# Reciprocal square roots by a power on GpSimd in a two-block transformer kernel

## The chip, the core and the metric

The kernel runs on one core of a Trainium2 chip, as one launch. The core has five engines, each with an instruction queue of its own that is worked off in order: TensorE (PE: matmuls and transposes into PSUM), VectorE (DVE), ScalarE (ACT), GpSimd (POOL) and SyncE (SP, which issues the DMAs). An instruction that needs another engine's result waits for it on a semaphore, and everything behind it in the same queue waits too. The metric is the device time in microseconds, the median of several runs.

## What is computed

One sequence of 256 tokens with 1024 features passes two blocks in float32. The first block puts 16 learned tokens ahead and mixes by a gated convolution branch and a sparse attention branch, followed by an FFN with a short convolution:

```python
h = rms_norm(stream, mix_norm_g[l])
...
y_a = conformer_conv_branch(u_conv, conv_ln_g[l], conv_ln_b[l], conv_dw_w[l], ...)   # has a layer norm
y_b = dsa_sparse_attention(q, k, v, q_idx, k_idx, w_idx, attn_w_o[l])
stream = stream + (g_a * y_a + g_b * y_b) @ w_merge_out[l]
h = rms_norm(stream, ffn_norm_g[l])
...
out = rms_norm(stream, final_norm_g)
```

The second block has two layers. The first mixes by gated linear attention (GLA: four heads, each with a norm of its own over 256 features), the second by block attention (MoBA). Each mixer and each FFN is added to a scaled stream and followed by a layer norm, so there are four of those:

```python
def layer_norm_2(x, g, b, eps=1e-5):
    xf = x.astype(jnp.float32)
    mu = jnp.mean(xf, -1, keepdims=True)
    var = jnp.mean(jnp.square(xf - mu), -1, keepdims=True)
    return ((xf - mu) * lax.rsqrt(var + eps) * g + b).astype(x.dtype)
```

Every norm thus needs 1/sqrt(v + eps) for one number per token (or per token and head).

## The kernel before

**Matmuls.** Each float32 matmul is split into a high and a low part of both factors, and three products are summed (high-high, high-low, low-high). The weights stream in chunks of 1 MB: SP issues their DMAs into three raw buffers (L111), ScalarE rounds each half chunk to its high part (`whi`, L134), DVE subtracts to get the low part (`wlo`, L136, 306 times). Activations stand transposed (features on partitions) in `hT_h` and `hT_l`; a norm's result is transposed on PE by `to_T` (L256, its PE line is L260), four 128x128 pieces at a time, copied out by ScalarE as the high part (L263) and subtracted by DVE for the low part (L266). `xs_late` (L836) is a projection that takes the high part's products first (L840, L841) and those with the low part last (L843), so that it can start before the low part is there.

**Order.** A scheduler sets the order of each engine's instructions by priorities and an estimate of when their inputs are there. Inside `tc.manual_schedule` the order on DVE and ScalarE is that of the code instead; the order on PE is the scheduler's everywhere. For the four layer norms of the second block the order is written out in the table `ORDER` (L65 to L70), one string each. An upper-case letter is a step on token tile 0, a lower-case one on tile 1: A adds stream and mixer (L742), S takes statistics of a half (L745), G joins them to mean and variance, adds epsilon and starts the root (L754, L755 and the first three rows of the iteration), C centres a half and multiplies by the gain (L749: y, the mean and the row `lg`), N is one Newton step, F finishes a half (times the root, plus the row `lb`, L761) and issues its transposes, L takes a low part (L266), x starts the next projection, t loads a ScalarE table, k lets weight splits go on. Digits are halves of 512 features.

**The root.** `rsqrt_steps` (L232) works on DVE: a shift and a subtraction of the integer bits give a first guess (L235, L236), L237 halves the negative argument, and three Newton steps refine it, each of two instructions for one column (L241, L245) or three for more columns (L243 to L245): 9 or 12 instructions of at most 128x3 numbers. It is used 17 times:
- at the start for the input norm, three columns (L307, L308); its readers scale the two token tiles on DVE (L311, L312) and ScalarE (L313), and PE transposes them;
- in `rstd_row` (L567), for the norm behind the convolution and for the FFN norm: PE sums over features (L572), DVE adds epsilon (L574), the root is taken (L575) and PE transposes it to a row (L578);
- in the final norm of the first block, once for each token tile (L714, L715); its reader L720 scales a half straight out of PSUM, and `to_T` follows;
- four times in the GLA mixer, two heads each (L1017, L1018), read by L1021;
- in the four layer norms, twice each.

## Time and profile before

| | |
|---|---|
| time, median of 3 runs | 1108.08 us (1105.93, 1108.08, 1108.15) |
| span of the profiled execution | 1106.3 us |
| PE busy | 1086.0 us (98%) |
| DVE busy | 767.1 us (69%) |
| ScalarE busy | 595.8 us (54%) |
| GpSimd busy | 0.2 us, four instructions |
| HBM read | 182.91 MB, 166 GB/s over the span |

The profile shows one execution. The page gives no time of its own for it besides the span; the median of the runs is 1.8 us above the span. Busy time counts an engine's instructions; PE's are pipelined, so that a start is more exact than an end. In a timeline the bracket behind a row is the time in which its engine had nothing to do before it, with the instruction that ended that wait.

### The profile page before, as it was taken

What the parts mean: (1) busy time and instruction counts of PE and PEld (TensorE: products, weight loads), DVE (VectorE), ACT (ScalarE), POOL (GpSimd) and SP (SyncE); (2) the same over time, 40 slices, a digit from 0 to 9 for tenths busy, and PEclk for the clock granted to TensorE, in tenths of its full rate; (3) what the DMA queues carried; (4) which work ended last, traced back from release to release, by engine and by line L of the source; (5) the groups of instructions that cost most, each with busy time, mean ns of one, the idle gap of its engine ahead of it and who ended that gap; (6) DMA issues with size and microseconds to landing.
All of it is one profiled execution on the core that took longest, in us unless ns stands there. A gap on an engine that the chain in (4) does not pass through costs nothing.

```text
span 1106.3 us, 17667 instructions
## 1 busy us (share of the span) xinstructions
PE 1086.0 (98%) x7022; PEld 972.8 (88%) x7022; DVE 767.1 (69%) x1494; ACT 595.8 (54%) x1049; POOL 0.2 (0%) x4
## 2 busy tenths in 40 slices
PE   8999999999999999999999999999999999999996
PEld 7999888999999999977877899999878878999995
DVE  6899999885677676865677745557675677555556
ACT  7785577664455555656452544446166925444440
POOL 0000000000000000000000000000000000000000
PEclk8999999999999999999999999999999999999999
DMA  7643136264265455545424555557264336555531
GB/s 279 242 145 124 45 111 212 93 211 154 94 210 190 161 199 178 187 162 177 162 94 173 195 188 188 190 191 265 78 228 153 142 125 228 191 182 183 180 141 39
DMA packets 27797, 185.10 MB, mean 167 GB/s; under 512 B 3473, under 2 KB 3857, under 8 KB 6466
## 3 DMA queue, kind: packets, MB, share of 16 engines
q1 hardware_dynamic: 27714, 183.97, 47.7%
q8 instruction: 55, 0.90, 0.3%
q14 instruction: 28, 0.23, 0.1%
HBM read 182.91 MB, written 1.05 MB: 166 GB/s over the span
## 4 chain that ended last, share of the span: by engine, by line
PE 88%; DVE 8%; ACT 2%; issue 1%; DMA 0%; SPq 0%; DVEq 0%; ACTq 0%
PE ps_wk L178 11%; PE ps_wk L179 11%; PE ps_wk L177 11%; PE ps_acc L183 10%; PE ps_acc L185 10%; PE ps_acc L184 10%; PE ps_acc L199 4%; PE ps_acc L177 3%; PE ps_acc L179 3%; PE ps_acc L178 3%; DVE wlo L136 1%; PE ps_wk L260 1%; PE ps_wk L511 1%; DVE yc L370 1%; PE ps_acc L840 1%
## 5 line engine op out<-in xcount | busy, mean ns | idle before, releaser
L136 DVE TENSOR_TENSOR wlo<-wraw,whi 128x1024 fp32r<-128x1024 f32 x306 | 371.5, 1223 | 209.6 <-ACT whi L134 208.9
L134 ACT ACTIVATE whi<-wraw 128x1024 fp32r<-128x1024 f32 x308 | 322.5, 1060 | 306.6 <-PE ps_wk L178 120.3
L178 PE MATMUL ps_wk<-hT_l,whi 128*128 128x256 f32 (+1 forms) x976 | 275.3, 282 | 0.0
L179 PE MATMUL ps_wk<-hT_h,wlo 128*128 128x256 f32 (+1 forms) x976 | 275.0, 282 | 0.0
L177 PE MATMUL ps_wk<-hT_h,whi 128*128 128x256 f32 (+1 forms) x976 | 274.3, 281 | 0.0
L177 PEld LDWEIGHTS ps_wk<-hT_h,whi 128*128 128x128 f32 x976 | 184.7, 189 | 1.0
L179 PEld LDWEIGHTS ps_wk<-hT_h,wlo 128*128 128x128 f32 x976 | 185.0, 190 | 0.4
L178 PEld LDWEIGHTS ps_wk<-hT_l,whi 128*128 128x128 f32 x976 | 184.1, 189 | 1.4
L183 PE MATMUL ps_acc<-whi,rg_h 128*128 128x512 f32 x328 | 131.5, 401 | 0.0
L184 PE MATMUL ps_acc<-wlo,rg_h 128*128 128x512 f32 x328 | 129.4, 394 | 0.0
L185 PE MATMUL ps_acc<-whi,rg_l 128*128 128x512 f32 x328 | 126.7, 394 | 0.0
L185 PEld LDWEIGHTS ps_acc<-whi,rg_l 128*128 128x128 f32 x328 | 61.6, 188 | 15.5 <-DVE rg_l L208 0.2
L183 PEld LDWEIGHTS ps_acc<-whi,rg_h 128*128 128x128 f32 x328 | 61.7, 188 | 13.7 <-ACT rg_h L206 0.2
L184 PEld LDWEIGHTS ps_acc<-wlo,rg_h 128*128 128x128 f32 x328 | 61.6, 188 | 12.7
L183 PE MATMUL ps_acc<-whi,hT_h 128*128 128x512 f32 (+1 forms) x184 | 71.5, 389 | 0.0
L185 PE MATMUL ps_acc<-whi,hT_l 128*128 128x512 f32 (+1 forms) x184 | 70.9, 385 | 0.0
L184 PE MATMUL ps_acc<-wlo,hT_h 128*128 128x512 f32 (+1 forms) x184 | 70.7, 384 | 0.0
L177 PE MATMUL ps_acc<-hT_h,whi 128*128 128x272 f32 (+2 forms) x240 | 69.3, 289 | 0.0
L178 PE MATMUL ps_acc<-hT_l,whi 128*128 128x272 f32 (+2 forms) x240 | 68.5, 286 | 0.0
L179 PE MATMUL ps_acc<-hT_h,wlo 128*128 128x272 f32 (+2 forms) x240 | 68.4, 285 | 0.0
L370 DVE SCALAR_TENSOR_TENSOR yc<-hp,dwh,yc 128x258 f32<-128x258 f32 (+14 forms) x140 | 60.8, 474 | 0.1
L368 ACT ACTIVATE z<-hp,dwh 128x258 f32<-128x258 f32 (+16 forms) x100 | 45.4, 498 | 14.5 <-DVE yc L372 10.9
(941 smaller groups left out, 1663.1 us busy)
## 6 DMA issues: line engine op xcount, KB each, us to landing
wraw<-in_wts_dram SPq DMA_DIRECT2D x166, 1024.0 KB, 4.9
lg<-in_rows_dram SPq DMA_DIRECT2D x4, 512.0 KB, 3.9
lb<-in_rows_dram SPq DMA_DIRECT2D x4, 512.0 KB, 3.9
x<-in_x_dram SPq DMA_DIRECT2D x2, 512.0 KB, 4.2
wraw<-in_wts_dram SPq DMA_DIRECT2D x2, 512.0 KB, 7.0
out_dram<-x SPq DMA_DIRECT2D x4, 256.0 KB, 2.0
mraw<-in_misc_dram SPq DMA_DIRECT2D x1, 576.0 KB, 12.7
tabs<-in_cst_dram SPq DMA_DIRECT2D x1, 544.0 KB, 12.0
```

Of the source, the lines that this page charges most:

```text
L134: A.activation(hi, r, AF.Copy)
L136: V.tensor_sub(lo, r, hi.bitcast(F32))
L177: PE.matmul(ps, wh, xh, start=first, stop=False)
L178: PE.matmul(ps, wh, xl, start=False, stop=False)
L179: PE.matmul(ps, wl, xh, start=False, stop=last)
L183: PE.matmul(ps, xh, wh, start=first, stop=False)
L184: PE.matmul(ps, xh, wl, start=False, stop=False)
L185: PE.matmul(ps, xl, wh, start=False, stop=last)
L199: PE.matmul(ps, w[:, k * P:(k + 1) * P], xT[2][:, k, a:b], start=k == 0, stop=k == KT - 1)
L260: PE.transpose(pt[:, a, :], src[:, k * P:(k + 1) * P], ident)
L368: A.activation(z[:, b, :], src[:, b, :], AF.Copy, scale=wc)
L370: V.scalar_tensor_tensor(dst[:, b, :], src[:, b, :], wc, dst[:, b, :], op0=OP.mult, op1=OP.add)
```

## The change

One function `rsqrt` takes the place of the iteration. DVE adds epsilon (with the factor 1/n where the input is a sum), and one GpSimd instruction raises the column to the power -0.5, with a constant tile of -0.5 as the second factor. The uses at the start, in the final norm, in the GLA mixer and in the layer norms go through it; `rstd_row` keeps its two epsilon rows and calls the power itself. In the table of orders all Newton steps fall away, so both centre passes of a tile stand behind its G.

```diff
@@ -63,15 +63,14 @@
 OHOLD = 0
 OG = ((0, 4), (4, 4))
 ORDER = (
-    "A0 S0 A1 S1 G C0 N N C1 N a0 F0 F1 s0 a1 L0 s1 L1 g x n c0 n n c1 f0 f1 l0 l1 k x",
-    "A0 S0 A1 S1 G N C0 N C1 N F0 F1 a0 L0 s0 L1 a1 s1 x g c0 n n c1 n f0 f1 t l0 l1 k x",
-    "A0 S0 A1 S1 G N C0 N C1 t N a0 F0 F1 a1 s0 L0 s1 L1 x g n c0 n c1 n f0 f1 l1 l0 k x",
-    "A0 S0 A1 S1 G N C0 N N F0 C1 F1 a0 s0 a1 s1 g c0 n n n c1 f0 f1",
+    "A0 S0 A1 S1 G C0 C1 a0 F0 F1 s0 a1 L0 s1 L1 g x c0 c1 f0 f1 l0 l1 k x",
+    "A0 S0 A1 S1 G C0 C1 F0 F1 a0 L0 s0 L1 a1 s1 x g c0 c1 f0 f1 t l0 l1 k x",
+    "A0 S0 A1 S1 G C0 C1 t F0 F1 a0 a1 s0 L0 s1 L1 x g c0 c1 f0 f1 l1 l0 k x",
+    "A0 S0 A1 S1 G C0 C1 F0 F1 a0 s0 a1 s1 g c0 c1 f0 f1",
 )
 PLAIN = set(range(30, 44))
 EARLY = (166, 236 - TAIL, 264)
 EARLY_SET = {e + i for e in EARLY for i in range(4)}
-MAGIC_RS = float(0x5F3759DF)
 
 
 @with_exitstack
@@ -221,6 +220,8 @@
     eps_t = per.tile([P, 2], F32, name="eps_t")
     V.memset(eps_t[:, 0:1], EPS)
     V.memset(eps_t[:, 1:2], EPS_LN2)
+    mhalf = per.tile([P, 4], F32, name="mhalf")
+    V.memset(mhalf, -0.5)
     ones = per.tile([P, P], F32, name="ones")
     V.memset(ones, 1.0 / D)
     hT = (per.tile([P, KT, L], F32R, name="hT_h"), per.tile([P, KT, L], F32R, name="hT_l"))
@@ -229,24 +230,13 @@
     def vcol(name, i):
         return vecs[:, VEC[name] + i:VEC[name] + i + 1]
 
-    def rsqrt_steps(v, n=1, rows_=P):
-        t = sc.tile([P, 24], F32, name="rs_t", tag="rs_t", bufs=4)
-        r, h, q = (t[:rows_, 8 * i:8 * i + n] for i in range(3))
-        V.tensor_scalar(q.bitcast(I32), v.bitcast(I32), 1, None, op0=OP.logical_shift_right)
-        V.tensor_scalar(r.bitcast(I32), q.bitcast(I32), -1.0, MAGIC_RS, op0=OP.mult, op1=OP.add)
-        V.tensor_scalar(h, v, -0.5, None, op0=OP.mult)
-        for _ in range(3):
-            yield r
-            if n == 1:
-                V.scalar_tensor_tensor(q, r, h, r, op0=OP.mult, op1=OP.mult)
-            else:
-                V.tensor_mul(q, r, r)
-                V.tensor_mul(q, q, h)
-            V.scalar_tensor_tensor(r, q, 1.5, r, op0=OP.add, op1=OP.mult)
-        yield r
-
-    def rsqrt_cols(v, n=1, rows_=P):
-        return [*rsqrt_steps(v, n, rows_)][-1]
+    def rsqrt(r, v, mul, eps):
+        if mul != 1.0:
+            V.tensor_scalar(v, v, mul, eps, op0=OP.mult, op1=OP.add)
+        else:
+            V.tensor_scalar(v, v, eps, None, op0=OP.add)
+        nc.gpsimd.tensor_tensor(r, v, mhalf[:, :r.shape[-1]], op=OP.pow)
+        return r
 
     def row_bcast(pool, src, n, tag, bufs):
         t = pool.tile([P, n], F32, name=tag, tag=tag, bufs=bufs)
...
-        V.tensor_scalar(ss[:, 0:3], ss[:, 0:3], 1.0 / D, EPS, op0=OP.mult, op1=OP.add)
-        rs = rsqrt_cols(ss[:, 0:3], 3)
+        rs = rsqrt(sc.tile([P, 4], F32, name="rs", tag="st", bufs=6)[:, 0:3], ss[:, 0:3], 1.0 / D, EPS)
...
-        r = rsqrt_cols(st[:, 0:3], 3)
+        r = sc.tile([P, 4], F32, name="rs", tag="st", bufs=6)[:, 0:3]
+        nc.gpsimd.tensor_tensor(r, st[:, 0:3], mhalf[:, 0:3], op=OP.pow)
...
-            V.tensor_scalar(st[:, 2:3], st[:, 2:3], 1.0 / D, EPS, op0=OP.mult, op1=OP.add)
-            r = rsqrt_cols(st[:, 2:3])
+            r = rsqrt(st[:, 3:4], st[:, 2:3], 1.0 / D, EPS)
...
             V.bn_aggr(st[:, 0:2], self.bs)
-            V.tensor_scalar(st[:, 2:3], st[:, 1:2], EPS_LN2, None, op0=OP.add)
-            self.newton = rsqrt_steps(st[:, 2:3])
-            self.r = next(self.newton)
+            self.r = rsqrt(st[:, 2:3], st[:, 1:2], 1.0, EPS_LN2)
...
-            elif op == "n":
-                next(self.newton)
...
-                V.tensor_scalar(st[:, :, 1], st[:, :, 0], 1.0 / 256, EPS, op0=OP.mult, op1=OP.add)
-                r = rsqrt_cols(st[:, :, 1], 2)
+                r = rsqrt(st[:, :, 1], st[:, :, 0], 1.0 / 256, EPS)
```

DVE's list has 1002 rows instead of 1185, GpSimd's has 26 instead of 7: 17 powers, one more instruction ahead of the first of them, and one branch fewer in the list. PE's order changes too, since the scheduler expects the roots at other times: the transposes of the root in the convolution's norm stand 11 rows behind its sums instead of 59, and in the FFN norm behind 6 instead of 20 of the identity matmuls of L702. (The file of the changed kernel has other line numbers: a power is L238 or L565, the epsilon row L235 or L237, the transposes of `to_T` L250, and `xs_late` is L825, L826 and L828.)

**DVE, LayerNorm 0, tile 1.** From the joining of the statistics (BN_AGGR) on; `rs_t` is the tile of the iteration, `lg` the gain row. Before:

```order
L754 BN_AGGR st_6399<-bs 128x2
L755 TENSOR_SCALAR st_6399<-st_6399 128x1
L235 TENSOR_SCALAR rs_t<-st_6399 128x1
L236 TENSOR_SCALAR rs_t<-rs_t 128x1
L237 TENSOR_SCALAR rs_t<-st_6399 128x1
L241 SCALAR_TENSOR_TENSOR rs_t<-rs_t 128x1
L245 SCALAR_TENSOR_TENSOR rs_t<-rs_t 128x1
L749 SCALAR_TENSOR_TENSOR y<-y,st_6399,lg 128x512
L241 SCALAR_TENSOR_TENSOR rs_t<-rs_t 128x1
L245 SCALAR_TENSOR_TENSOR rs_t<-rs_t 128x1
L241 SCALAR_TENSOR_TENSOR rs_t<-rs_t 128x1
L245 SCALAR_TENSOR_TENSOR rs_t<-rs_t 128x1
```

and in the changed kernel, with the two rows ahead of BN_AGGR, up to the finishing passes (L748):

```order
L734 BN_STATS bs<-y 128x6
L256 TENSOR_TENSOR hT_l<-ps_wk,hT_h 128x4x128
L743 BN_AGGR st_6302<-bs 128x2
L738 SCALAR_TENSOR_TENSOR y<-y,st_6302,lg 128x512 x2
L237 TENSOR_SCALAR st_6302<-st_6302 128x1
L748 SCALAR_TENSOR_TENSOR x_87<-y,st_6302,lb 128x512 x2
```

Here the epsilon row now stands behind both centre passes; in the other seven tiles of the layer norms it stands ahead of them.

**PE, final norm, tile 1.** The transposes of the scaled tile (`x`, two groups of four) and the products with the low part of tile 0 (`hT_l`). Before:

```order
L840 MATMUL ps_acc<-whi,hT_h 128x512
L841 MATMUL ps_acc<-wlo,hT_h 128x512
L843 MATMUL ps_acc<-whi,hT_l 128x512 x7
L260 MATMUL ps_wk<-cs,x_85 128x128 x4
L843 MATMUL ps_acc<-whi,hT_l 128x512
L260 MATMUL ps_wk<-cs,x_85 128x128 x4
L840 MATMUL ps_acc<-whi,hT_h 128x512
L841 MATMUL ps_acc<-wlo,hT_h 128x512
```

and now:

```order
L825 MATMUL ps_acc<-whi,hT_h 128x512
L826 MATMUL ps_acc<-wlo,hT_h 128x512
L250 MATMUL ps_wk<-cs,x_87 128x128 x4
L828 MATMUL ps_acc<-whi,hT_l 128x512
L250 MATMUL ps_wk<-cs,x_87 128x128 x4
L828 MATMUL ps_acc<-whi,hT_l 128x512 x7
L825 MATMUL ps_acc<-whi,hT_h 128x512
L826 MATMUL ps_acc<-wlo,hT_h 128x512
```

The first group of transposes has moved ahead of all eight products with the low part.

**PE, LayerNorm 2, tile 0.** The end of the FFN (`rg_h`, `rg_l`), the transposes, and the first products of the MoBA projection (`we_qk`). Before:

```order
L183 MATMUL ps_acc<-whi,rg_h 128x512
L184 MATMUL ps_acc<-wlo,rg_h 128x512
L185 MATMUL ps_acc<-whi,rg_l 128x512
L183 MATMUL ps_acc<-whi,rg_h 128x512
L184 MATMUL ps_acc<-wlo,rg_h 128x512
L185 MATMUL ps_acc<-whi,rg_l 128x512
L260 MATMUL ps_wk<-cs,x_84 128x128 x8
L840 MATMUL ps_wk<-we_qk_9139,hT_h 128x512
```

and now:

```order
L183 MATMUL ps_acc<-wlo,rg_h 128x512
L184 MATMUL ps_acc<-whi,rg_l 128x512
L250 MATMUL ps_wk<-cs,x_86 128x128 x8
L182 MATMUL ps_acc<-whi,rg_h 128x512
L183 MATMUL ps_acc<-wlo,rg_h 128x512
L184 MATMUL ps_acc<-whi,rg_l 128x512
L182 MATMUL ps_acc<-whi,rg_h 128x512
L183 MATMUL ps_acc<-wlo,rg_h 128x512
L184 MATMUL ps_acc<-whi,rg_l 128x512
L825 MATMUL ps_wk<-we_qk_9006,hT_h 128x512
```

The eight transposes have moved ahead of the FFN's last six products. In LayerNorm 0 they have moved in the same way by three products on tile 0 and by one on tile 1, and in LayerNorm 1 by six on each tile; in LayerNorm 2 they stay at the end on tile 1. In the final norm's tile 0 they come one product earlier.

## Rows read from the trace of the kernel before

**Rows 1.** The page, parts 1 and 4: busy time, share of the span and instructions of each engine; and the chain of work that ended last, by engine.

```profile
PE 1086.0 (98%) x7022; PEld 972.8 (88%) x7022; DVE 767.1 (69%) x1494; ACT 595.8 (54%) x1049; POOL 0.2 (0%) x4
...
PE 88%; DVE 8%; ACT 2%; issue 1%; DMA 0%; SPq 0%; DVEq 0%; ACTq 0%
```

**Rows 2.** The start of the kernel: timeline of DVE (the row that adds epsilon, and the last Newton step), of ScalarE (the scaling of the second token tile and the first weight split), of SP's queue (issue of the first half of the first weight chunk), and the list of DMA issues in 2.9 to 3.3 us (KB of one, median us from issue to landing). Timeline rows here and below: start us, us, engine, line, operation, out<-in, shape, count, and in brackets the idle time before it and what ended that.

```profile
7.36 0.17 DVE L307 TENSOR_SCALAR ss<-ss 128x3 f32<-128x3 f32 x1
9.54 0.16 DVE L245 SCALAR_TENSOR_TENSOR rs_t<-rs_t 128x3 f32<-128x3 f32 x1
...
9.79 1.34 ACT L313 ACTIVATE xn<-x,rs_t 128x512 f32<-128x512 f32 x2 [2.79 <-DVE rs_t L245]
11.04 1.04 ACT L134 ACTIVATE whi<-wraw 128x1024 fp32r<-128x1024 f32 x1
...
3.06 0.43 SPq L111 DMA_DIRECT2D wraw<-in_wts_dram  x1
...
wraw<-in_wts_dram SPq DMA_DIRECT2D x1, 512.0 KB, 6.6
```

**Rows 3.** The final norm of the first block: timeline of DVE (epsilon row and scaled halves of tile 0), of PE (transposes of tile 0), of DVE (epsilon row of tile 1), of PE (the low-part matmuls ahead of the transposes of tile 1).

```profile
476.81 0.15 DVE L714 TENSOR_SCALAR st<-st 128x1 f32<-128x1 f32 x1
478.78 1.41 DVE L720 SCALAR_TENSOR_TENSOR x<-ps_acc,rs_t,yc 128x512 f32<-128x512 f32 x2
...
479.68 0.63 PE L260 MATMUL ps_wk<-cs,x 128*128 128x128 f32 x4 [0.18 <-DVE x L720]
...
487.77 0.15 DVE L714 TENSOR_SCALAR st<-st 128x1 f32<-128x1 f32 x1
...
488.91 1.80 PE L843 MATMUL ps_acc<-whi,hT_l 128*128 128x512 f32 x7
```

**Rows 4.** Timeline of GpSimd (POOL) in 0 to 2 us, its last instruction of the span; of ScalarE in 204 to 234 us, a small copy out of PSUM; and of ScalarE at the start, a load of its function table.

```profile
0.33 0.10 POOL L1252 MEMSET const-uint8-127<- 128x1 uint8 x1
...
209.21 0.27 ACT L504 ACTIVATE pT<-ps_wk 16x128 f32<-16x128 f32 x1 [0.32 <-PE ps_wk L502]
...
0.72 1.28 ACT L277 ACT_TABLE_LOAD   x1 [0.72 <-PEq L1252]
```

**Rows 5.** The norm behind the convolution: timeline of DVE (its two epsilon rows), and of PE (two neighbouring matmuls, and the transposes of the root).

```profile
221.28 0.20 DVE L574 TENSOR_SCALAR st<-ps_wk 128x2 f32<-128x2 f32 x2
...
228.02 0.28 PE L177 MATMUL ps_acc<-oT_h,whi 128*128 128x258 f32 x1
228.14 0.28 PE L178 MATMUL ps_acc<-oT_l,whi 128*128 128x258 f32 x1
228.45 0.57 PE L578 MATMUL ps_wk<-cs,rs_t 128*128 128x128 f32 x3
```

**Rows 6.** The FFN norm of the first block: timeline of DVE (its two epsilon rows), and of PE (the identity matmuls ahead of the transposes, and the first matmul of the FFN).

```profile
290.21 0.21 DVE L574 TENSOR_SCALAR st<-ps_wk 128x2 f32<-128x2 f32 x2 [0.82 <-PE ps_wk L572]
...
290.11 2.50 PE L702 MATMUL ps_acc<-cs,s 128*128 128x128 f32 x20
...
294.26 0.39 PE L194 MATMUL ps_wk<-hT_h,whi 128*128 128x258 f32 x1 [0.39 <-ACT hT_h L640]
```

**Rows 7.** LayerNorm 0: timeline of DVE (epsilon row and finishing passes of tile 0, variance of tile 1) and of PE (the transposes of tile 0 and of tile 1).

```profile
601.13 0.15 DVE L755 TENSOR_SCALAR st<-st 128x1 f32<-128x1 f32 x1
604.66 1.41 DVE L761 SCALAR_TENSOR_TENSOR x<-y,rs_t,lb 128x512 f32<-128x512 f32 x2
...
608.96 0.20 DVE L754 BATCH_NORM_AGGREGATE st<-bs 128x2 f32<-128x12 f32 x1
...
605.46 1.38 PE L260 MATMUL ps_wk<-cs,x 128*128 128x128 f32 x8 [0.46 <-DVE x L761]
...
613.15 1.29 PE L260 MATMUL ps_wk<-cs,x 128*128 128x128 f32 x8 [0.53 <-DVE x L761]
```

**Rows 8.** Busy time of the engines in the stretch in which the four head norms of the GLA mixer lie, with the count of instructions of each, the granted clock, the DMA share and GB/s.

```profile
545.00:575.00 30.00, 30.00 (x150) 21.50 (x148) 21.79 (x85) 11.48 (x28) 0.00 (x0) 1.00 0.24 76
```

**Rows 9.** LayerNorm 1: timeline of DVE (epsilon rows of tiles 0 and 1) and of PE (their transposes).

```profile
789.24 0.15 DVE L755 TENSOR_SCALAR st<-st 128x1 f32<-128x1 f32 x1
...
798.73 0.16 DVE L755 TENSOR_SCALAR st<-st 128x1 f32<-128x1 f32 x1
...
793.10 0.66 PE L260 MATMUL ps_wk<-cs,x 128*128 128x128 f32 x4
...
802.58 1.32 PE L260 MATMUL ps_wk<-cs,x 128*128 128x128 f32 x8
```

**Rows 10.** LayerNorm 2: timeline of DVE (epsilon row of tile 0, add of tile 1's second half, epsilon row of tile 1) and of PE (the transposes of tile 0 and of tile 1).

```profile
902.27 0.15 DVE L755 TENSOR_SCALAR st<-st 128x1 f32<-128x1 f32 x1
...
907.12 0.68 DVE L742 SCALAR_TENSOR_TENSOR y<-x,ps_acc 128x512 f32<-128x512 f32 x1
...
910.34 0.15 DVE L755 TENSOR_SCALAR st<-st 128x1 f32<-128x1 f32 x1
...
906.69 1.29 PE L260 MATMUL ps_wk<-cs,x 128*128 128x128 f32 x8 [0.56 <-DVE x L761]
...
914.29 1.29 PE L260 MATMUL ps_wk<-cs,x 128*128 128x128 f32 x8 [0.44 <-DVE x L761]
```

**Rows 11.** LayerNorm 3, behind the last matmul: timeline of DVE (epsilon row and finishing passes of tile 1).

```profile
1098.79 0.15 DVE L755 TENSOR_SCALAR st<-st 128x1 f32<-128x1 f32 x1
1101.84 1.41 DVE L761 SCALAR_TENSOR_TENSOR x<-y,rs_t,lb 128x512 f32<-128x512 f32 x2
```

## The prediction

> **What bounds the kernel now.** I read the times first, then the first and fourth parts of the page: PE is busy 98% of the span, and the chain of work that ended last runs through PE for 88% of it and through DVE for 8% [rows 1]. So a shorter DVE saves time only where PE waits for it, where DVE alone stands between the inputs and the first matmul, and behind the last matmul. The change takes 183 of 1185 instructions from DVE's list (17 uses of the iteration, each of 9 or 12 small instructions), and nearly all of that lies under a busy PE. So I went to each of the 17 uses in order of time, and read on DVE when the epsilon row ends and when the result is first used, on PE whether it waited there, and from the order of the instructions whether PE now reaches the place earlier than before.
>
> **The unknown.** Call X the time from the end of the epsilon row to the start of the instruction that reads the root: a hand-off to GpSimd, the power, and a hand-off back. Before, these steps take 2.3 us at the start (from 7.53, the end of the row that adds epsilon, to 9.79) and 1.8 us in the final norm (476.96 to 478.78) [rows 2, 3]. No row shows GpSimd computing anything but four start-up memsets of 0.10 us [rows 4]. From below: a power as short as such a memset and two hand-offs of 0.09 (from the end of the last Newton step at 9.70 to ScalarE's start at 9.79 [rows 2]) give X = 0.28; nothing below that is possible, since the hand-offs remain. From above: the longest single item of an otherwise idle engine here is ScalarE's table load of 1.28 us; two of these (a logarithm and an exponential) with the hand-offs make 2.76 [rows 4]. I take a logarithm, a product and an exponential as three small passes at ScalarE's 0.27 us each [rows 4], 0.8 in all, plus 0.2 of hand-offs: X = 1.0. That is an estimate, nearer the lower end because the tiles are as small as the memsets.
>
> **Place by place, at X = 1.0, against the profiled span of 1106.28.**
> *Start.* The root was read at 9.79, and will be at 7.53 + 1.0 = 8.53: -1.2, rounded down. ScalarE's two passes and then its first weight split queue behind the root; the first half chunk was issued at 3.06 and lands 6.6 later, at 9.66, and the split started at 11.04 [rows 2]. So the gain ends at 1.4, and 1.2 is still inside it.
> *Conv norm.* The transposes of the root stand 48 rows earlier on PE; rows there start 0.12 apart, so PE reaches them at 228.45 - 5.8 = 222.6. The epsilon rows end at 221.48, the root is there at 222.48 [rows 5]: 0.
> *FFN norm.* The epsilon rows end at 290.42, the root comes at 291.42; PE reaches the transposes after 6 instead of 20 identity matmuls of 0.125 (290.11 + 0.75 = 290.86) and waits for 0.6. Behind it stand 0.57 of transposes and 18 x 0.125: 294.24, and the next projection started at 294.26 [rows 6]: 0.
> *Final norm.* Tile 0: root at 477.96, first scaled half 0.90 later for PE (478.78 to 479.68) at 478.86. PE stood still 0.18 there and now comes by one matmul earlier without a wait: -0.2. Tile 1 is the price of the new order: the transposes stand ahead of all eight low-part matmuls, where before seven went first. PE comes by at 488.91; the scaled half is ready at 487.92 + 1.0 + 0.9 = 489.82 [rows 3]. PE waits 0.9, and behind it, in its own queue, stand the eight matmuls that were its work before: +0.9.
> *LayerNorm 0.* Both centre passes now stand directly behind the epsilon row, some 1.4 together (as the two finishing passes of their size, 1.41), and hide X. Tile 0: 601.28 + 1.4 + 0.7 for an add = 603.4, for PE at 604.2 (lag 0.80); PE's place is three matmuls (0.7) before 605.00, at 604.30. The wait of 0.46 goes. Tile 1 has its epsilon row behind the centres, so nothing hides the power: 608.96 + 0.20 + 1.4 + 0.15 + 1.0 + 0.9 = 612.61, PE's place is 612.39, one matmul earlier; of the wait of 0.53 it keeps 0.2: -0.3 [rows 7]. Together -0.8.
> *GLA heads.* Four powers, whose readers on DVE hold up weight splits queued behind them. PE was busy for 30.00 of the 30 us around them [rows 8]: 0, up to X = 2.76 by the same cover.
> *LayerNorm 1.* Centres end at 789.39 + 1.4; PE's place is six matmuls of 0.23 before 793.10, at 791.7, the half is ready at 791.6. Tile 1: 798.89 + 1.4 + 0.8 = 801.1 against 801.2, as far before 802.58 [rows 9]. 0, with 0.1 to spare at both.
> *LayerNorm 2.* Tile 0: ready at 902.42 + 1.4 + 0.9 = 904.72; PE's place, six matmuls before 906.13, is 904.73: the wait of 0.56 goes. The six then end the FFN at 907.4, so the add of tile 1's second half starts at 907.5 instead of 907.12 and its epsilon row ends 0.4 later, at 910.9; with centres and lag 913.2, when PE is due at 913.27. The wait of 0.44 goes too [rows 10]: -1.0.
> *LayerNorm 3*, all behind the last matmul: 1098.94 + 1.4 = 1100.34 instead of 1101.84 [rows 11]: -1.5.
> Sum: -1.2 - 0.2 + 0.9 - 0.8 - 1.0 - 1.5 = -3.8, a span of 1102.5. The median of the runs is 1108.08, 1.8 above the profiled span; at that distance the forecast is **1104.3 us**.
>
> **The two ends.** At X = 0.28 the start gains its full 1.4, the FFN norm 0.6, tile 1 of the final norm loses 0.2 only, LayerNorm 0 gains 1.0: -5.5, 1102.6. At X = 2.76 the start loses 0.6, conv norm 1.6, FFN norm 1.7, final norm 1.2 + 2.7, LayerNorm 0 1.5, LayerNorm 1 twice 1.25, LayerNorm 2 1.6, and the end gains 0.1: +13, 1121. The early places on PE make it steep: the same sum at X = 1.6 is zero.
>
> **Rivals.**
> *The shared port.* Each centre pass reads two arrays from SBUF (y and the gain row), and the power reads SBUF too. If these exclude each other, the power waits for both centres, and X behind the epsilon row becomes 1.4 + 1.0 = 2.4 in LayerNorm 1 to 3 and tile 0 of LayerNorm 0; nothing is hidden. Then LayerNorm 0 gives -0.6, LayerNorm 1 costs 0.9 twice, LayerNorm 2 +0.9 (places 1.0 late), the end -0.5: sum +1.0, **1109.1**, no change. For it speaks that the new order sets the two side by side at seven of eight LayerNorm tiles; no row of before has GpSimd and DVE busy together, so nothing speaks against it. The Trainium skill (SBUF — State Buffer, "Who interferes with whom") states this as a rule: a DVE instruction with two SBUF inputs contends with a GpSimd one that reads SBUF, by a lock held for the whole instruction. No run here shows it yet.
> *Code for the power, fetched at the first use.* GpSimd's list of the changed kernel has one more instruction ahead of its first power, besides the powers. If it fetches something only when the first power is called, the price is a transfer, by the nearest row 6.6 (the first half chunk of weights [rows 2]); the root at the start is then read at 7.53 + 6.6 + 1.0 = 15.1 instead of 9.79, so +5.4 stands where I have -1.2: sum +2.8, **1110.9**, slower. A delay of 3.8 turns the sum, one of 6.0 makes it slower by 0.2%. Against it: GpSimd is idle from 0.4 to 7.5 [rows 4], and a fetch that starts then is done in time. The Trainium skill (GPSIMD Engine Reference, "2.1 Instruction dispatch") has about 6 us, measured 5.95, for the first call of freshly loaded code; by that figure the time would be 1110.2 us.
> *A slow power.* Any X over 1.6, with the upper end 1121; by a line from zero at 1.6 to +13 at 2.76 the time is slower by more than 0.2% (2.2 us) from X = 1.8.
> That GpSimd doesn't run the power at all is excluded: its list has 17 of them.
>
> **Chances.** Forecast, X up to 1.25 (by a line from -3.8 at 1.0 to zero at 1.6 the point at which the gain falls to 2.2): 0.50, 1101 to 1106. X from 1.25 to 1.8 without a lock: 0.10, no change. The lock, of which the rows of before show neither that it is there nor that it isn't: 0.20, three quarters of it no change and the rest slower. The late fetch: 0.08, slower for the most part. X over 1.8: 0.12, slower. Runs of the same kernel spread over 0.2% (1105.93 to 1108.15), so within 0.2% (1105.9 to 1110.3) counts as no change: faster 0.50, same 0.28, slower 0.22. The range is 1101 to 1111: below it X would have to be under its lower bound, above it lie most of the slow power and part of the late fetch.
>
> **What would show it.** POOL's tensor-tensor rows give the power itself, and the gap from epsilon row to reader gives X. In the final norm PE should wait some 0.9 at the transposes of tile 1, released by the scaling on DVE. In LayerNorm 1 and 2 the finishing pass should follow the second centre at once, and PE should have no wait; if it starts a full power after the centres, the lock holds. At the start the first scaling should begin near 8.5; near 15, the fetch was late. I am wrong if X exceeds 1.6, or if PE waits in places where I count none.

## The result, and the profile after

The changed kernel takes 1099.4 us (median of 4 runs, 1099.13 to 1100.74) against 1108.12 us before (1105.93 to 1108.15): a ratio of 0.9926, with a 95% interval of 0.9912 to 0.9940. That is 8.7 us faster. I had forecast 1104.3 us, so the direction was right, the size was not, and the time lies below the range of 1101 to 1111. The profiled execution has a span of 1097.3 us, 9.0 less than the one before.

The page of the kernel after, its parts 1 and 4:

```profile
span 1097.3 us, 17545 instructions
PE 1080.9 (99%) x7022; PEld 969.7 (88%) x7022; DVE 743.2 (68%) x1321; ACT 595.5 (54%) x1049; POOL 13.8 (1%) x21
...
PE 91%; DVE 5%; ACT 2%; issue 1%; DMA 0%; POOL 0%; SPq 0%; DVEq 0%; ACTq 0%; POOLq 0%
```

PE is busy 5.1 us less than in [rows 1], and the chain goes through DVE for 5% instead of 8%. GpSimd's timeline has the powers themselves: three columns at the start and in the FFN norm, one column in the final norm, two in the GLA heads, one in layer norms 1 and 3.

```profile
7.62 0.86 POOL L238 TENSOR_TENSOR rs<-ss,mhalf 128x3 f32<-128x3 f32 x1 [7.18 <-DVE ss L235]
...
286.75 0.85 POOL L565 TENSOR_TENSOR rs<-st,mhalf 128x3 f32<-128x3 f32 x1 [67.58 <-DVE st L563]
...
484.17 0.55 POOL L238 TENSOR_TENSOR st<-st,mhalf 128x1 f32<-128x1 f32 x1 [10.95 <-DVE st L235]
...
552.59 0.70 POOL L238 TENSOR_TENSOR st<-st,mhalf 128x2 f32<-128x2 f32 x1 [67.86 <-DVE st L235]
...
784.58 0.98 POOL L238 TENSOR_TENSOR st<-st,mhalf 128x1 f32<-128x1 f32 x1 [176.91 <-DVE st L237]
...
1091.72 0.92 POOL L238 TENSOR_TENSOR st<-st,mhalf 128x1 f32<-128x1 f32 x1 [7.49 <-DVE st L237]
```

One column takes 0.55 us where DVE is idle, 0.91 to 0.99 beside the centre passes; two take 0.70, three 0.85 or 0.86. The start, which answers to [rows 2]: DVE's epsilon row, ScalarE's first reader of the root, PE's first transposes.

```profile
7.30 0.17 DVE L235 TENSOR_SCALAR ss<-ss 128x3 f32<-128x3 f32 x1
...
8.51 1.34 ACT L302 ACTIVATE xn<-x,rs 128x512 f32<-128x512 f32 x2 [1.57 <-POOL rs L238]
...
9.09 0.39 PE L310 MATMUL ps_wk<-cs,xn 16*128 16x16 f32 x4 [1.77 <-issue]
```

From the end of the epsilon row at 7.47 to the reader at 8.51 is X = 1.04 for three columns, where I had taken 1.0. With one column it is shorter. Layer norm 0, tile 1, where nothing hides the power (DVE: epsilon row, first finishing pass):

```profile
606.88 0.15 DVE L237 TENSOR_SCALAR st<-st 128x1 f32<-128x1 f32 x1
607.70 0.75 DVE L748 SCALAR_TENSOR_TENSOR x<-y,st,lb 128x512 f32<-128x512 f32 x1 [0.67 <-POOL st L238]
```

From 607.03 to 607.70: X = 0.67. PE's waits for the two tiles of the final norm, which answer to [rows 3]:

```profile
474.16 0.63 PE L250 MATMUL ps_wk<-cs,x 128*128 128x128 f32 x4 [0.71 <-DVE x L709]
...
485.66 0.52 PE L250 MATMUL ps_wk<-cs,x 128*128 128x128 f32 x3 [0.49 <-DVE x L709]
```

And the transposes of layer norm 0 tile 0, of layer norm 1 tile 1 and of layer norm 2 tile 0, each with PE's next matmul, which answer to [rows 7, 9, 10]:

```profile
601.03 1.17 PE L250 MATMUL ps_wk<-cs,x 128*128 128x128 f32 x8
601.95 0.47 PE L182 MATMUL ps_acc<-whi,rg_h 128*128 128x512 f32 x1
...
796.09 1.20 PE L250 MATMUL ps_wk<-cs,x 128*128 128x128 f32 x8
797.05 0.48 PE L828 MATMUL ps_acc<-we_qkT,hT_l 128*128 128x512 f32 x1
...
899.08 1.27 PE L250 MATMUL ps_wk<-cs,x 128*128 128x128 f32 x8
900.11 0.48 PE L182 MATMUL ps_acc<-whi,rg_h 128*128 128x512 f32 x1
```

PE has no idle time ahead of them, as forecast for tile 0 of layer norms 0 and 2. What the reader should note for later is the distance from the first transpose to the next matmul, 0.92, 0.96 and 1.03. In the kernel before, the next matmul after the same three groups of [rows 7, 9, 10] starts here:

```profile
606.80 0.50 PE L840 MATMUL ps_wk<-we0h,hT_h 128*128 128x512 f32 x1
...
803.93 0.51 PE L840 MATMUL ps_acc<-we_qkT,hT_h 128*128 128x512 f32 x1
...
908.01 0.50 PE L840 MATMUL ps_wk<-we_qk,hT_h 128*128 128x512 f32 x1
```

From 605.46, 802.58 and 906.69 that is 1.34, 1.35 and 1.32.

### The profile page after: what moved, and what is told of

It is laid out like the page before. It is cut to its first block, busy times and chain, and to the rows that moved or that the text cites. A ratio compares the mean times of both kernels' runs of the same rounds, so it can differ in the third digit from the quotient of the medians.

```text
span 1097.3 us, 17545 instructions
## 1 busy us (share of the span) xinstructions
PE 1080.9 (99%) x7022; PEld 969.7 (88%) x7022; DVE 743.2 (68%) x1321; ACT 595.5 (54%) x1049; POOL 13.8 (1%) x21
## 3 DMA queue, kind: packets, MB, share of 16 engines
HBM read 182.91 MB, written 1.05 MB: 168 GB/s over the span
## 4 chain that ended last, share of the span: by engine, by line
PE 91%; DVE 5%; ACT 2%; issue 1%; DMA 0%; POOL 0%; SPq 0%; DVEq 0%; ACTq 0%; POOLq 0%
PE ps_wk L178 11%; PE ps_wk L177 11%; PE ps_wk L176 11%; PE ps_acc L182 10%; PE ps_acc L184 10%; PE ps_acc L183 10%; PE ps_acc L176 4%; PE ps_acc L178 4%; PE ps_acc L177 4%; PE ps_acc L198 4%; PE ps_wk L250 1%; DVE wlo L135 1%; PE ps_wk L500 1%; PE ps_acc L828 1%; PE ps_wk L498 1%
## 5 line engine op out<-in xcount | busy, mean ns | idle before, releaser
L183 PEld LDWEIGHTS ps_acc<-wlo,rg_h 128*128 128x128 f32 x328 | 61.7, 188 | 12.9
```

Source lines behind the costliest of these rows:

```text
L183: PE.matmul(ps, xh, wl, start=False, stop=False)
```

## Experiments

Two explanations for the missing 4.9 us stood against each other at first. The places where the root is waited for might each give more than I counted; or something that is not the power might have changed with it. One thing pointed to the second: comparing the start of the same matmuls in the two traces, the changed kernel gained 2.0 us near 131 us, where no norm lies. There PE waited for a copy of the attention's queries (`q`), and the granted clock fell behind the wait in the kernel before. Rows of before: PE's wait, and the stretch behind it (columns: us, then busy time and instructions of PE, PEld, DVE, ACT, POOL, then the granted clock, the DMA share, GB/s).

```profile
130.86 0.26 PE L521 MATMUL ps_wk<-kT,q 128*8 128x16 f32 x4 [2.03 <-DVE q L519]
...
130.00:135.00 5.00, 4.14 (x15) 3.34 (x16) 4.83 (x15) 4.07 (x9) 0.00 (x0) 0.68 0.07 18
```

The same of the kernel after:

```profile
129.21 0.26 PE L510 MATMUL ps_wk<-kT,q 128*8 128x16 f32 x4 [1.68 <-DVE q L508]
...
130.00:135.00 5.00, 5.00 (x25) 3.94 (x23) 4.84 (x16) 4.68 (x12) 0.00 (x0) 1.00 0.13 21
```

The clock records of before put the lower of the two levels, 1.2 GHz, at 131.8 to 135.2 us. They have such a half-clock stretch at the start as well, at 12.3 to 19.1 us (6.8 long); in the changed kernel it lies at 9.5 to 12.9 (3.4 long).

**The power in one place only.** Two kernels split the change, both made from the kernel before with the tile of -0.5 and the function `rsqrt` added: the power at the start alone, and the power in the four layer norms alone (with the new table of orders).

```diff
 a_start
-        V.tensor_scalar(ss[:, 0:3], ss[:, 0:3], 1.0 / D, EPS, op0=OP.mult, op1=OP.add)
-        rs = rsqrt_cols(ss[:, 0:3], 3)
+        rs = rsqrt(sc.tile([P, 4], F32, name="rs", tag="st", bufs=6)[:, 0:3], ss[:, 0:3], 1.0 / D, EPS)
```

> The kernel before with the power at the start alone; all other uses keep the Newton iteration. If the places add up, the matmuls from 20 us on come 1.6 us earlier (the root read 1.3 earlier, the rest from the clock) and the time falls by 1.3 to 1.6, to about 1106.6. If the half-clock stretch near 131 us hangs on the wait there, which is 0.35 shorter once the start is earlier, it goes too and the time falls by 3.3, to 1104.8. Rival: the start is paced by the weight DMAs, then PE is at most 0.5 earlier at 20 us and the time 1107.6 or more.

1105.57 us against 1108.02, ratio 0.9977 (0.9968 to 0.9987): 2.5 us. ScalarE reads the root at 8.81 instead of 9.79, 0.98 earlier; the matmuls from 20 us on come 0.84 earlier, not 1.6, those from 100 us on 0.54, and those from 140 us on 2.58: the half-clock stretch near 131 is gone. The one at the start is still 6.8 us long.

```diff
 b_ln
-            V.tensor_scalar(st[:, 2:3], st[:, 1:2], EPS_LN2, None, op0=OP.add)
-            self.newton = rsqrt_steps(st[:, 2:3])
-            self.r = next(self.newton)
+            self.r = rsqrt(st[:, 2:3], st[:, 1:2], 1.0, EPS_LN2)
```

> The kernel before with the power in the four layer norms alone, with the new table of orders. If the eight transposes cost PE 0.9 when both halves are ready and 1.3 to 1.9 when they wait for them (hidden in rows that show no idle time), the four places give -1.4, -0.6, -1.5 and -1.6, together -5.1: about 1103.0. Rival: only the idle time that the rows show is won, -1.0, 0, -1.0, -1.5, together -3.5: about 1104.6. The half-clock stretch near 131 us should stay as in the kernel before.

1100.78 us, ratio 0.9937 (0.9924 to 0.9949): 7.2 us. The matmuls behind layer norm 0 come 1.43 earlier than those ahead of it, behind layer norm 1 0.65, behind layer norm 2 1.50, as expected by the first explanation. But 2.1 more are there at 140 us already, with the start unchanged, so that the time is 2.2 below the expected 1103.0. So my guess that the earlier start does away with the stretch at 131 us fell too.

**Neither start nor power.** The two kernels share one small thing with the changed one, the memset of the tile of -0.5.

```diff
 i_memset
+    mhalf = per.tile([P, 4], F32, name="mhalf")
+    V.memset(mhalf, -0.5)
     ones = per.tile([P, P], F32, name="ones")
```

> The kernel before with one small memset more on DVE at the start (the tile of -0.5, which nothing reads) and no power. Both kernels with the power in one place only had lost a wait of 0.36 on DVE near 95 us, the wait of PE near 129 us was 0.4 shorter, and the half-clock stretch at 131 us was gone, though nothing of theirs lies near. If that comes with any shift of the instructions or addresses and not from the power, this kernel loses it too: about 1106.0. Rival: it needs the power, then 1108.0.

1106.49 us against 1107.94, ratio 0.9987 (0.9979 to 0.9996). No power, and the stretch is gone. Its rows (PE's wait, and the same window):

```profile
130.84 0.26 PE L523 MATMUL ps_wk<-kT,q 128*8 128x16 f32 x4 [1.69 <-DVE q L521]
...
130.00:135.00 5.00, 4.16 (x22) 3.65 (x23) 4.84 (x16) 4.09 (x9) 0.00 (x0) 1.00 0.10 33
```

The wait is 1.69 instead of 2.03, the clock 1.00 instead of 0.68. Every other kernel run here also has the memset, and none has the stretch near 131 us; whether any other small change would do the same as the memset was not tried. Of the 45 runs of the kernel before that were timed beside these experiments, 41 took 1107.32 to 1108.72 us at a mean clock of 0.991 to 0.993, and four took 1106.20 to 1106.27 at 0.995 or 0.996. So the stretch may now and then be missing in that kernel too; no trace of such a run was kept. Why the wait is longer in the kernel before can be followed back to DVE near 95 us: its rows there, and those of the kernel with the memset.

```profile
94.98 0.29 DVE L438 MAX8 m<-sco 128x8 f32<-128x128 f32 x1
95.53 0.48 DVE L431 SCALAR_TENSOR_TENSOR sco<-r,wix,sco 128x256 f32<-128x256 f32 x1 [0.26 <-DVE m L438]
```

```profile
95.29 0.30 DVE L440 MAX8 m<-sco 128x8 f32<-128x128 f32 x1
95.50 0.48 DVE L433 SCALAR_TENSOR_TENSOR sco<-r,wix,sco 128x256 f32<-128x256 f32 x1
```

The same two instructions in the same order, 0.55 apart and 0.21 apart; DVE, busy from there to the copy of `q` but for two waits that both kernels have, doesn't make up for the 0.34. The bracket names DVE's own preceding instruction, which explains the order and not the delay; what delayed it I have not found. In the traces the same matmuls are 0.3 later than in the kernel before from 20 us on, behind a longer half-clock stretch at the start (10.2 us against 6.8), and 1.7 earlier from 140 us on: 2.0 at the place itself, 1.5 in time.

**Where a tile lies.** In the trace of the changed kernel the matmuls of conv projection and FFNs come 0.04 to 0.05 earlier with every 20 us than in the kernel before, mostly on a smooth slope, 1.3 over the span. The kernels with the power at the start or in the layer norms alone have no such slope; they also still have the iteration's tile `rs_t`.

```diff
 k_pad
         V.memset(ss, 1.0)
+        pad = sc.tile([P, 24], F32, name="pad", tag="pad", bufs=4)
+        V.memset(pad, 0.0)
```

> The changed kernel with an unused tile of the size of the iteration's (four buffers of 24 numbers) in the same pool, and a memset of it. In the changed kernel the matmuls of the FFNs come 0.05 us earlier with every 20 us, 1.3 us over the span, and in the kernels that still have the iteration's tile they don't. If that comes from the tile's place in SBUF, this kernel loses it: about 1100.7. Rival: it comes from something else, then 1099.4.

1101.40 us (1101.07 to 1101.68), ratio 0.9941 (0.9928 to 0.9955): 2.0 slower than the changed kernel. In the traces the span is 2.6 longer. About 1.3 of it is the slope, which is gone. 0.7 is there from 20 us on: 0.26 of that stands already in DVE's epsilon row (7.56 against 7.30), the rest comes behind a half-clock stretch of 6.8 us at the start instead of 3.4. Another 0.3 arises at 408 us, and I did not follow it up. The other direction, from the kernel before:

```diff
 n_lay (i_memset with the iteration's columns elsewhere)
-        t = sc.tile([P, 24], F32, name="rs_t", tag="rs_t", bufs=4)
-        r, h, q = (t[:rows_, 8 * i:8 * i + n] for i in range(3))
+        r, h, q = (sc.tile([P, 4], F32, name="st", tag="st", bufs=6)[:rows_, :n] for _ in range(3))
```

> The kernel before with the unread memset, and with the three columns of the Newton iteration in tiles that the pool has anyway, so that its own tile of four buffers is gone from SBUF; no power. If the small gain of the FFN matmuls hangs on where tiles lie, this kernel is 1.3 faster than the one with the memset alone: 1105.2. Rival: it needs the power or the rest of the change, then 1106.5.

1104.89 us against 1108.14, ratio 0.9973 (0.9963 to 0.9984): 1.6 less than with the memset alone, 0.2 of it at the start, where the half-clock stretch is 6.8 us instead of 10.2. Two matmuls far apart in the same FFN, in the kernel with the memset alone and in this one (PE):

```profile
625.08 0.28 PE L178 MATMUL ps_wk<-hT_l,whi 128*128 128x256 f32 x1
...
775.08 0.28 PE L179 MATMUL ps_wk<-hT_h,wlo 128*128 128x256 f32 x1
```

```profile
624.18 0.28 PE L178 MATMUL ps_wk<-hT_l,whi 128*128 128x256 f32 x1
...
773.86 0.28 PE L179 MATMUL ps_wk<-hT_h,wlo 128*128 128x256 f32 x1
```

150.00 and 149.68 us for the same work, with no wait in between. This kernel has the Newton iteration everywhere and is 3.2 us faster than the kernel before.

**The power against the clean base.** The changed kernel was run again on the same chip:

> The changed kernel again, on the same chip as the three above: 1099.1 to 1100.7 as before.

1099.96 us (1099.29 to 1100.28), so the power itself is worth 4.9 us against the 1104.89 of the kernel with the iteration, and 5.6 from profiled span to profiled span (1103.1 to 1097.5; the profiled run of the changed kernel, at 1099.33, is 0.6 below the median). Between these two traces there is no slope and no difference near 131 us; they differ in the half-clock stretch at the start (6.8 us against 3.4). The shift of the same matmul ahead of and behind each place can be read off:

| place | same matmul, iteration | power | shift so far | this place | forecast |
|---|---|---|---|---|---|
| start (seen behind a wait for ScalarE at 88) | 100.10 | 98.88 | -1.22 | -1.2 | -1.2 |
| convolution's norm | 250.08 | 248.75 | -1.33 | -0.1 | 0 |
| FFN norm | 460.07 | 458.29 | -1.78 | -0.45 | 0 |
| final norm | 500.10 | 499.11 | -0.99 | +0.8 | +0.7 |
| GLA heads | 590.21 | 589.79 | -0.42 | +0.6 | 0 |
| layer norm 0 | 640.12 | 638.29 | -1.83 | -1.4 | -0.8 |
| layer norm 1 | 830.15 | 827.70 | -2.45 | -0.6 | 0 |
| layer norm 2 | 940.21 | 936.24 | -3.97 | -1.5 | -1.0 |
| layer norm 3, to the end | 1103.1 | 1097.5 | -5.6 | -1.6 | -1.5 |

**Does the sum hang on X?** Every power is taken twice into the same place.

```diff
 h_pow2
         nc.gpsimd.tensor_tensor(r, v, mhalf[:, :r.shape[-1]], op=OP.pow)
+        nc.gpsimd.tensor_tensor(r, v, mhalf[:, :r.shape[-1]], op=OP.pow)
...
         nc.gpsimd.tensor_tensor(r, st[:, 0:3], mhalf[:, 0:3], op=OP.pow)
+        nc.gpsimd.tensor_tensor(r, st[:, 0:3], mhalf[:, 0:3], op=OP.pow)
```

> The changed kernel with every power taken twice in a row into the same place. If the sum goes by the way from the epsilon row to the reader, each place pays what its cover doesn't hide: start, convolution and FFN norm 0.86 each, final norm 0.55 twice, layer norm 0 0.55 on tile 1, and layer norms 1 to 3 0.25 on each tile that ends late: +5.0 to 5.5, 1104.4 to 1104.9. Rival: the second power waits for the second centre pass too, then layer norms 1 to 3 pay 0.7 a tile and it is 1107 or more. If the power were hidden nearly everywhere, under 1102.

1108.84 us, ratio to the kernel before 1.0008 (0.9999 to 1.0017): the whole gain is gone, which is steeper than I expected (1104.4 to 1104.9). The span is 1107.3, 10.0 more than with one power, and the same matmuls in the two traces show where: 1.1 at the start, 1.0 in the convolution's norm, 2.6 in the FFN norm, 0.8 in the final norm, 1.1 in the GLA heads, 0.6, 1.05, 1.1 and 0.6 in layer norms 0 to 3. Layer norms 1 and 2 thus pay about half a microsecond a tile and not 0.25, and the FFN norm pays 2.6 and not 0.9. The time, over 1107, is what the rival gave, a second power that waits for the second centre pass; but the tiles of layer norms 1 and 2 pay 0.5 and not its 0.7, and most of the excess is that of the FFN norm and of the GLA heads, where I had none. In the FFN norm PE's wait grew from 0.43 to 1.36, and the clock fell behind it (PE's row in the changed kernel; in the kernel with two powers the row, and the window):

```profile
287.65 0.57 PE L568 MATMUL ps_wk<-cs,rs 128*128 128x128 f32 x3 [0.43 <-POOL rs L565]
```

```profile
290.77 0.43 PE L570 MATMUL ps_wk<-cs,rs 128*128 128x128 f32 x2 [1.36 <-POOL rs L567]
...
290.00:295.00 5.00, 4.23 (x22) 4.04 (x22) 3.61 (x10) 3.10 (x9) 0.72 (x1) 0.66 0.00 0
```

**What holds up the power beside DVE.** A first try put the add (one input from SBUF) between the epsilon row and the centre passes in layer norms 0 and 2.

```diff
 g_addfirst
-    "A0 S0 A1 S1 G C0 C1 a0 F0 F1 ..."
+    "A0 S0 A1 S1 G a0 C0 C1 F0 F1 ..."
...
-    "A0 S0 A1 S1 G C0 C1 t F0 F1 a0 a1 ..."
+    "A0 S0 A1 S1 G a0 C0 C1 t F0 F1 a1 ..."
```

> The changed kernel, with the add of tile 1's first half (one input from SBUF, one from PSUM) set between the epsilon row and the centre passes (two inputs from SBUF) of tile 0 in layer norms 0 and 2. If a DVE instruction with two SBUF inputs holds up the power, the power takes 0.55 in these two places, as it does alone, and stays near 0.95 in the other layer norms. Rival: any busy DVE holds it up, then it stays near 0.95 in both. The time should stay within 0.6 of the changed kernel's: 1099.4 to 1100.0.

1099.43 us (0.9922, 0.9909 to 0.9936), and the power took 0.55 and 0.54 in the two places, 0.92 to 0.98 in the others. But the add waited 0.95 for its matmuls, so DVE stood still beside the power: this told nothing. The second try has DVE busy with one input from SBUF:

```diff
 j_stats
-    "A0 S0 A1 S1 G C0 C1 F0 F1 ... x g c0 c1 ..."
+    "A0 S0 A1 S1 G S0 S1 C0 C1 F0 F1 ... x g s0 s1 c0 c1 ..."
```

> The changed kernel with two repeated statistics passes (one input from SBUF each, no change of the result) between the epsilon row and the centre passes in layer norm 1, both tiles. If it is the second SBUF input of the centre passes that holds up the power, it takes 0.55 here and stays near 0.95 in layer norms 2 and 3. Rival: any busy DVE holds it up, then near 0.95 here too. The time may rise by up to 2.6, since two passes of 0.65 are added ahead of the transposes twice.

GpSimd's rows of layer norm 1, both tiles, and of layer norm 2, tile 0, in that kernel:

```profile
784.92 0.54 POOL L238 TENSOR_TENSOR st<-st,mhalf 128x1 f32<-128x1 f32 x1 [176.91 <-DVE st L237]
...
794.26 0.54 POOL L238 TENSOR_TENSOR st<-st,mhalf 128x1 f32<-128x1 f32 x1 [8.80 <-DVE st L237]
...
897.36 0.92 POOL L238 TENSOR_TENSOR st<-st,mhalf 128x1 f32<-128x1 f32 x1 [102.56 <-DVE st L237]
```

0.54 beside the statistics, 0.92 beside the centre passes. The time was 1099.42 and 1100.84 us, in two runs only, about that of the changed kernel (1099.13 to 1100.74). In the traces the matmuls behind layer norm 1 are no later than those ahead of it: the scheduler had set PE's transposes later as well, so the added passes cost nothing.

**A better version.** The power costs time in the final norm and in the GLA heads. The first kernel with the iteration back in these two places has the tile `rs_t` again:

```diff
 c_hybrid (the changed kernel with the iteration in two places)
-            r = rsqrt(st[:, 3:4], st[:, 2:3], 1.0 / D, EPS)
+            V.tensor_scalar(st[:, 2:3], st[:, 2:3], 1.0 / D, EPS, op0=OP.mult, op1=OP.add)
+            r = rsqrt_cols(st[:, 2:3])
...
-                r = rsqrt(st[:, :, 1], st[:, :, 0], 1.0 / 256, EPS)
+                V.tensor_scalar(st[:, :, 1], st[:, :, 0], 1.0 / 256, EPS, op0=OP.mult, op1=OP.add)
+                r = rsqrt_cols(st[:, :, 1], 2)
```

> The changed kernel, with the Newton iteration again in the final norm and in the GLA heads, where matmuls came 0.78 and 0.56 later than their neighbours ahead. If the power's new places on PE cost that, the time falls by 1.3, to 1098.1. Rival: the Newton chain is 1.0 longer than the power on the way to the transposes, which takes the same back: 1099.4 or more.

1099.91 us (0.9928, 0.9914 to 0.9941), no gain: against the changed kernel its trace wins 0.8 in the final norm and 0.2 in the GLA mixer, and loses about 1.4 on the slope, which is gone, and 0.2 at the start. The last but one has the same edit and the iteration's columns in the tiles that the pool has anyway:

```diff
 l_best (c_hybrid, and)
-        t = sc.tile([P, 24], F32, name="rs_t", tag="rs_t", bufs=4)
-        r, h, q = (t[:rows_, 8 * i:8 * i + n] for i in range(3))
+        r, h, q = (sc.tile([P, 4], F32, name="st", tag="st", bufs=6)[:rows_, :n] for _ in range(3))
```

> The changed kernel with the Newton iteration in the final norm and the GLA heads alone, its columns in tiles that the pool has anyway. If the places on PE and the place in SBUF add up, it keeps the small gain of the FFN matmuls and wins 0.8 in the final norm and 0.2 to 0.5 in the GLA mixer against the changed kernel: 1098.2 to 1098.4. Rival: the tile's absence is not what makes the difference, then 1099.9 as in the first version of this kernel.

1098.77 us (1098.59 to 1099.61), ratio 0.9918 (0.9904 to 0.9931): 1.2 less than the changed kernel on the same chip, the fastest median of all. In the traces the two places give 0.7 and 0.6, and the span is 0.8 shorter, since 0.3 is lost at the start (a half-clock stretch of 6.8 us against 3.4) and 0.2 near 860 us. The last one adds matmuls ahead of the first transposes:

```diff
 l_warm (l_best, and)
-WARM = 16
+WARM = 24
```

> The same with 24 instead of 16 matmuls on ones ahead of the first transposes, which shortens PE's wait there from 1.5 to some 0.4 us. If the half-clock stretch at the start hangs on that wait and PE sets the pace there, 0.3 to 0.7 are won against the kernel with 16; rival: ScalarE's copies set the pace, no difference.

Its profile has no half-clock stretch at the start at all, the matmuls from 20 us on come 0.33 earlier, and the span is 1096.4 instead of 1096.7. The runs however fall in two groups, 1098.14 and 1098.39, and 1100.06 to 1100.40, median 1100.06: whether it helps is not settled.

## Why the prediction was wrong in size

**The range rested on a wrong bound.** Its lower end was X = 0.28 in a sum over places, as if nothing but the power could change. Of the 8.7 us, 4.9 are the power's (the clean pair); by itself that gives about 1103.2 us, inside the range. The other part came with the change and not from the power: the unread memset alone takes 1.5 from the kernel before, and the iteration's tile, out of its place, another 1.6. These three make 8.0; the second set of runs of the changed kernel lies 8.2 below the kernel before, the first 8.7. The step that failed is the sum's silent assumption that a stretch in which no instruction of the change lies runs as before: it put such stretches at nothing, without a reason, and they gave 3.1. The trace of before had the half-clock stretch in its granted clock, and I had not asked what it hung on.

**The sum for the power was right in its mechanism, and partly by luck in its numbers.** It gave 3.8 where the clean pair shows 4.9 (5.6 between the profiled spans). X was 1.04 for three columns against 1.0, but 0.67 for one, where I made no difference between one column and three; layer norm 3 gave 1.6 (forecast 1.5). The start gave 1.2 as forecast, but in a trace whose half-clock stretch there is 3.4 us long. Where it stayed at 6.8, with the power at the start alone, the root was read 0.98 earlier and 0.54 of that was left at 100 us; the forecast had no such term. The final norm cost 0.8 (forecast 0.7), and that is luck too: inside it two errors met. The section on the change says that the transposes of tile 0 come one product earlier; it is seven, since the list repeats in threes and I took the wrong repeat. So PE waits 0.71 there where I had a gain of 0.2, while tile 1, with the shorter X, waits 0.49 and not 0.9. This wait in tile 0 is one of the prediction's own signs of being wrong: PE waiting where it counted none.

**The step that was mis-sized: what a group of eight transposes costs.** I counted as gain, at each layer norm, at most the idle time in the bracket of [rows 7, 10], and nothing in layer norm 1, where [rows 9] have none. In the kernel before, though, a group of eight and PE's next matmul hold two more waits. The first four transposes started when the first half was finished and the second four when the second was, 0.66 to 0.75 later. And the next matmul reads the half just transposed, so it stood until ScalarE had copied it: it starts 0.23 to 0.30 behind the last transpose. Both waits are missing in the brackets of PE's matmul rows, but they show in the rows of its weight loads (PEld), which the prediction leaves out. The list of PEld's waits (us in total, times, longest), before and after, and the row ahead of layer norm 1's next matmul in the kernel before:

```profile
PEld ps_wk L260 <- PE ps_wk L260: 1.0, 4, 0.3
PEld ps_wk L840 <- ACT hT_h L263: 1.0, 4, 0.3
...
803.93 0.19 PEld L840 LDWEIGHTS ps_acc<-we_qkT,hT_h 128*128 128x128 f32 x1 [0.26 <-ACT hT_h L263]
```

```profile
PEld ps_wk L825 <- ACT hT_h L253: 0.5, 2, 0.3
PEld ps_wk L250 <- PE ps_wk L250: 0.5, 2, 0.2
```

So the groups last 1.32 to 1.35 to the next matmul, against 0.92 to 1.03 in the changed kernel. There the transposes stand among matmuls that don't read the new half, and the next matmul follows the last transpose by 0.03. In tile 0 of layer norm 0 and in layer norm 1 the second four also follow sooner, 0.53 to 0.55 behind the first four's start; in tile 0 of layer norm 2 they still come 0.64 behind, so there only the wait for ScalarE went. Tile 1 of layer norm 2, whose transposes stay at the end, still takes 1.32. Layer norms 0, 1 and 2 give 0.6, 0.6 and 0.5 more than forecast, in two experiments alike (the power in the layer norms alone, and the clean pair); the distances in the rows shown account for 0.4, 0.4 and 0.3 of it.

**GLA was forecast at nothing and costs 0.6.** PE's busy share of 100% there [rows 8] did not cover it. DVE now stands idle for 0.81 to 0.88 ahead of each pair of scaled heads, while the power runs, and its product with the gate (`gs`), which feeds PE's transposes, stands behind all eight scaled heads, where with the iteration it stood behind five. PE waits 0.3 for it, in a place where it did not wait before:

```profile
562.35 0.63 PE L250 MATMUL ps_wk<-cs,gs 128*128 128x128 f32 x4 [0.29 <-DVE gs L1013]
```

The other 0.3 I have not followed up. The Newton iteration back in both this place and the final norm won 1.2 in the median. The FFN norm gave 0.45 where I had 0: PE waited 0.43 for the root, where I had 0.6, and the wait of 0.39 ahead of the FFN's first matmul [rows 6] is gone; I have not split it further.

**The rivals.** The shared port was half right. The power beside a centre pass takes 0.91 to 0.99 and not 0.55, and beside a pass with one input from SBUF it takes 0.54, which agrees with the rule of the Trainium skill (SBUF — State Buffer, "Who interferes with whom"). But it doesn't wait for both centre passes: in layer norm 1 it ends at 785.56, and the second pass ends at 785.81. The two passes together still last 1.40 with the power beside them, so all of it stays hidden:

```profile
784.41 1.40 DVE L738 SCALAR_TENSOR_TENSOR y<-y,st,lg 128x512 f32<-128x512 f32 x2
```

The late fetch didn't happen: the first power took 0.86, as long as the two later ones of three columns. The Trainium skill's 6 us for a first call of freshly loaded code (GPSIMD Engine Reference, "2.1 Instruction dispatch") appear in none of these rows. A slow power was not the case, but the kernel with two powers showed how steep that sum is: with 0.55 to 0.95 more at each place it stands 3.95 above the clean base of 1104.89, where one power stands 4.9 below it. The FFN norm's fall of the clock is part of that, and my line from zero at X = 1.6 had no such term.

## What to carry to other kernels

A change that moves a small chain from a busy engine to an idle one is worth what the waits for it give, and those are found place by place. For PE the idle time ahead of a group of matmuls is not all of it: the distance from the group's first instruction to the next one's start, and the waits of the weight loads, show what a merged row hides. Before a gain of under 1% is put down to the change, compare the same instructions in both traces along the whole span: a shift that arises where the change has no instruction belongs to something else, and a kernel with the change's side effects alone (its memset, its missing tile) shows how much. It doesn't show why: here neither cause was found. And an instruction list that a scheduler makes anew can give back part of a gain: two of nine places lost time, and putting them back was worth another 1.2 us in the median (0.8 from span to span).

## What I had not expected of the hardware

- PE's wait for `q` near 130 us lasted 1.56 to 1.69 in the changed kernel and the twelve experiments, with full clock behind it each time; in the kernel before it lasted 2.03, with a fall to 1.2 GHz for 3.4 us behind it. In the kernel with two powers a wait of 1.36 at 290 us had such a fall behind it, so the length of the wait alone doesn't decide.
- Removing or adding four buffers of 24 numbers in one pool changed the pace of matmuls in which nothing waits by 0.2% (150.00 against 149.68 us). Which address matters, and for which operand, was not tried.
- The same two instructions on DVE, in the same order, started 0.55 apart in the kernel before and 0.21 apart with one memset more at the start. The cause is open.
